# Gates and output products in pairs of pieces, in the order of the seven products

## The chip, the cores and the metric

One core of a Trainium2 chip runs the whole kernel. The metric is device microseconds of one execution; the median of the runs is compared.

## The reference

One inference step of a one-layer encoder trunk in float32, for 1024 prompt frames and 64 sample frames (1088 tokens) of width 1024:

```python
proj = xn @ w_in                                   # xn = rmsnorm(x), 1024 -> 5120
cb, cc, ch, q, k, v, ga, gb = jnp.split(proj, splits, axis=-1)
cv, conv_state = causal_conv(cc * ch, conv_prefix, w_conv)
ya = (cb * cv) @ w_conv_out                        # 512 -> 1024
o, new_k, new_v = attn_fn(heads(q), heads(k), heads(v))   # 8 heads of 64, chunk band
yb = o.reshape(B, L, ATT_DIM) @ w_attn_out         # 512 -> 1024
merged = jax.nn.sigmoid(ga) * ya + jax.nn.sigmoid(gb) * yb
x = x + merged @ w_out
x = x + (jax.nn.silu(h @ w1) * (h @ w3)) @ w2      # h = rmsnorm(x), 2816 hidden
return rmsnorm(x, g_final), ...
```

## The kernel before

Every float32 operand of a matmul is kept as two tiles of the fast format, a high part and the rest (`split`: a cast on ScalarE, then a subtraction on VectorE). A product is the sum of three matmuls: high weights by high data, high weights by the data's rest, the weights' rest by high data.

The 1088 tokens lie in columns: two halves of `HT` = 544 (512 prompt, 32 sample each), and each half is two pieces of `HN` = 272 columns, the width of one matmul. Channels are on the 128 partitions.

Most of the projection and the feed-forward go through `run`: a 2x2 block scheme with seven products instead of eight. It takes, for one block of weights, high weights by high data for both pieces of a half, high weights by the rest for both pieces, then the weights' rest by high data for both pieces (L266). Its operands are "quarter" tiles, in which a row block of 128 channels is `ROW` = 1152 floats long and the rest lies `HT + 8` = 552 floats behind the high part.

Twelve blocks of the two gates' projections (`GATES`: all eight of `ga` and the last four of `gb`) and the two output products `ya` and `yb` go through `product`, one piece of 272 columns at a time (L330 to L332). A gate has 8 row blocks, so 24 matmuls for a piece; an output has 4, so 12. `gate` copies each piece from PSUM (pool `pmm`, three banks) to a staging tile (`st_pool`, five) on ScalarE (L813), and GpSimd's queue stores it (L814).

The order of the program: the first halves of the first four gates (pieces 0 and 1), then the other pieces of these and five more gates, with about 2.7 steps of attention put between each two (`between`), then the last three gates (`LAST` = 3), when attention has ended. Ahead of these three the loads of `u` (the convolution branch) and `o` (attention, divided by its sums on VectorE and split into `ob`) are issued, and those of the gates. A planner that works through the program ahead of the run fixes the order of each engine's instructions: a later one may be placed ahead of one whose inputs or buffers it expects late. Gate matmuls stand singly among those of attention in the trace.

The outputs: for two blocks m of 128 channels `ya` (L1085 multiplies it by the sigmoid of `ga`), for the same two `yb` (L1095 multiplies, L1096 adds), and the sum is split into `mg` and, for the sample's columns, `ms`. Five banks of PSUM (`psum2`) hold pieces. Then the products with `w_out` follow, sample rows (from `ms`) first (L1143, L1144).

Weights: the high part lies in one of eight tiles of 512 (`ws`), the rest in one of eight slots of 512 in `low`, with an offset inside the slot (`at`): 0 for the gates and `run`, 40 for the outputs, 24 where the weights are the moving operand. `taken` counts the slots.

Of the kernel before, what the change touches and what calls it, by code (L numbers as in the profile page):

```python
# [8 lines left out]
F32 = mybir.dt.float32  # L9
# [46 lines left out]
class Acts:  # L56
# [3 lines left out]
        self.t = t  # L60

    def at(self, l, k, o, n):
        return self.t[:, l, k, o : o + n]


@with_exitstack
def encoder_kernel(ctx: ExitStack, tc: tile.TileContext, ins, outs):
# [58 lines left out]
    def split(hi, lo, src):  # L126

        a = act.copy(hi, src)  # L128
        b = vec.tensor_tensor(lo, src, hi.bitcast(F32), op=ALU.subtract)  # L129
        return a.ins, b.ins  # L130
# [192 lines left out]
    def product(out, w, x, o, n):  # L323

        kt = 4 * len(w)
        for k in range(kt):
            a, b = (t[:, k % 4] for t in w[k // 4])
            p, q = x.at(0, k, o, n), x.at(1, k, o, n)
            first, then = (q, p) if x is xn and o // HN % 2 == 0 else (p, q)
            mm(out, a, first, start=k == 0, stop=False)  # L330
            mm(out, a, then, start=False, stop=False)  # L331
            mm(out, b, p, start=False, stop=k == kt - 1)  # L332

    PIECES = [(j * HN, HN) for j in range(4)]
    GATES = [("a", m) for m in range(8)] + [("b", m) for m in range(4, 8)]
    for g, m in GATES:
# [468 lines left out]
    def gate(i, cs):  # L805
        g, m = GATES[i]
        dst = ga_d if g == "a" else gb_d
        for c in cs:
            o, n = PIECES[c]
            ps = pmm.tile([P, 512], F32, tag="mm", name=f"g{i}_{c}")  # L810
            product(ps[:, :n], gate_w[i], xn, o, n)
            st = st_pool.tile([P, HN], F32, tag="st", name=f"gst{i}_{c}")
            act.copy(st[:, :n], ps[:, :n])  # L813
            nc.gpsimd.dma_start(dst[m * P : (m + 1) * P, o : o + n], st[:, :n])  # L814
# [194 lines left out]
    sg = {}  # L1009

    def gates_in(nm, m):
        if nm == "gb":
            t = mp.tile([P, T], F32, tag="rc", name=f"gb{m}", bufs=3)
            nc.sync.dma_start(t, gb_d[m * P : (m + 1) * P])
            for o, n in PIECES:
                sg[nm, m, o] = t[:, o : o + n]
            return
        for o, n in PIECES:
            t = sg[nm, m, o] = mp.tile([P, HN], F32, tag=nm, name=f"{nm}{m}_{o}", bufs=8)
            nc.sync.dma_start(t, ga_d[m * P : (m + 1) * P, o : o + n])  # L1020

    head_load(0)

# [11 lines left out]
    for i in range(4, len(GATES)):  # L1035
        gate_w[i] = next_w()
        if i == len(GATES) - LAST:
            for _ in steps:
                pass
            att_stack.close()  # L1040
            uo = pg_stack.enter_context(tc.tile_pool(name="uo", bufs=1, reuse_waits="tile"))
            both_x = []
            for nm, pad in (("u", 56), ("ob", 48)):
                uo.tile([P, pad], F32, name=f"pad_{nm}")
                t = uo.tile([P, 2, 4 * T + 8], F32R, name=nm)[:, :, : 4 * T]
                both_x.append(Acts(t.rearrange("p l (k t) -> p l k t", k=4)))
            u, ob = both_x
            mp = pg_stack.enter_context(tc.tile_pool(name="mgp", bufs=4, reuse_waits="tile"))
            for k in range(4):
                if k == 3:  # L1050
                    gates_in("ga", 0)
                for q in {0: (0,), 1: (1,), 2: (), 3: (2, 3)}[k]:
                    nc.sync.dma_start(u.t[:, :, q].bitcast(F32), u_d[q])
                o = ob.t[:, 0, k].bitcast(F32)
                nc.sync.dma_start(o, o_d[k * P : (k + 1) * P])
                r = mp.tile([P, T], F32, tag="rc", name=f"rc{k}", bufs=3)
                for j in range(2):
                    src = rc_d[2 * k + j]
                    ld = nc.sync.dma_start(
                        r[j * HD : (j + 1) * HD], bass.AP(tensor=src.tensor, offset=src.offset, ap=[[0, HD], [1, T]])  # L1060
                    )
                vec.tensor_tensor(r, o, r, op=ALU.mult)
                split(ob.t[:, 0, k], ob.t[:, 1, k], r)
            with tc.issue_after(ld.ins):
                gates_in("ga", 1)
                gates_in("gb", 0)
        for c in range(4):
            gate(i, (c,))
            between()


    mg = quarters("mg")
    ms = mspool.tile([P, KD, 2, TS], F32R, tag="ms", name="ms")
    psum2 = pg_stack.enter_context(tc.tile_pool(name="psum2", bufs=5, space=PSUM, reuse_waits="tile"))
    for m0 in range(0, 8, 2):
        for m in (m0, m0 + 1):
            wa = next_w()
            if m0:
                gates_in("ga", m)
            for o, n in PIECES:  # L1080
# [4 lines left out]
                vec.tensor_tensor(t, ya[:, :n], t, op=ALU.mult)  # L1085
        for m in (m0, m0 + 1):
            wb = next_w()
            if m:
                gates_in("gb", m)
            for o, n in PIECES:  # L1090
                t, z = sg.pop(("ga", m, o)), sg.pop(("gb", m, o))
                act.activation(z, z, AF.Sigmoid)
                yb = psum2.tile([P, 512], F32, tag="mm", name=f"yb{m}_{o}")
                product(yb[:, :n], wb, ob, o, n)
                vec.tensor_tensor(z, yb[:, :n], z, op=ALU.mult)  # L1095
                vec.tensor_tensor(t, t, z, op=ALU.add)  # L1096
                split(mg.at(0, m, o, n), mg.at(1, m, o, n), t)
                h, a = o // HT, 512 - o % HT
                if a < n:
                    split(ms[:, m, 0, 32 * h : 32 * h + 32], ms[:, m, 1, 32 * h : 32 * h + 32], t[:, a:])  # L1100
    pg_stack.close()


# [62 lines left out]
    if True:  # L1166
# [557 lines left out]
```

## Time and profile before

| | |
|---|---|
| median of 3 runs | 1477.31 us (1476.44 to 1478.0) |
| the profiled execution | 1475.81 us, span 1473.8 us |
| granted TensorE clock | 0.999 |
| TensorE matmuls | 1458.0 us busy, 99% of the span, 10200 of them |
| VectorE, ScalarE, GpSimd busy | 979.2, 678.1, 133.1 us |
| HBM | 172.89 MB read, 91.92 MB written |

A matmul is shown with its whole way through the array, so that the next one starts before it ends; the distance from one start to the next tells what one costs. Lines name the kernel's source (L330 is line 330). Rows of the view by stretches give start and end in us, the length, then the busy time and number of instructions of each engine, the granted clock, the DMA engines' busy share and GB/s.

### The profile page before, as it was taken

The page shows a single profiled execution, that of the slowest core. Times are in us where ns is not written, and L with a number is a line of the kernel's source. Part 1 is how long each engine was busy: PE and PEld are TensorE (multiplying, and loading weights), DVE is VectorE, ACT ScalarE, POOL GpSimd, SP SyncE. Part 2 cuts the span into 40 slices and gives each one's busy share as a digit, 9 for nine tenths or more (in the row PEclk, how much of TensorE's full clock was granted, in tenths as well). Part 3 has the DMA queues.
Part 4 walks back from the last instruction along what each step waited for, and adds up shares of the span by engine and source line. Part 5 has one row for each costly group of instructions (what it writes and reads, how often), then busy time and mean ns, then how long its engine had stood idle before and what let it go on. Part 6 is the DMA issues. An engine that isn't in the chain of part 4 may idle for free.

```text
span 1473.8 us, 26481 instructions
## 1 busy us (share of the span) xinstructions
PE 1458.0 (99%) x10200; PEld 1369.7 (93%) x10200; DVE 979.2 (66%) x1850; ACT 678.1 (46%) x1396; POOL 133.1 (9%) x243
## 2 busy tenths in 40 slices
PE   8999999999999999999999999999999999999997
PEld 6899999999999999998889999999999999888886
DVE  7975465633776753763489767666666768957676
ACT  7644333434776753631355444444444445412223
POOL 1400010001111121000100111110011111000000
PEclk9999999999999999999999999999999999999999
DMA  8586523178766539544433454433344448777675
GB/s 292 177 271 224 177 93 113 60 212 233 190 191 176 152 101 326 186 126 136 147 114 108 147 183 162 161 140 120 119 149 159 149 161 308 256 233 248 212 268 203
DMA packets 164029, 264.72 MB, mean 180 GB/s; under 512 B 18624, under 2 KB 98688, under 8 KB 163872
## 3 DMA queue, kind: packets, MB, share of 16 engines
q1 hardware_dynamic: 143040, 196.13, 42.4%
q0 software_dynamic: 19712, 64.81, 12.2%
q10 hardware_dynamic: 1152, 2.10, 0.4%
q8 instruction: 80, 1.31, 0.4%
q14 instruction: 45, 0.37, 0.1%
HBM read 172.89 MB, written 91.92 MB: 180 GB/s over the span
## 4 chain that ended last, share of the span: by engine, by line
PE 92%; DVE 3%; DMA 2%; ACT 1%; SPq 1%; issue 1%; ACTq 0%; DVEq 0%
PE Ab L266 9%; PE Aa L266 8%; PE A L1637 8%; PE Db L266 4%; PE Da L266 4%; PE D L1637 4%; PE g L330 2%; PE g L331 2%; PE g L332 2%; PE B L1637 2%; PE Bb L266 2%; PE Ba L266 2%; PE wo L1139 2%; PE wo L1141 2%; PE wo L1140 2%; PE t L952 2%
## 5 line engine op out<-in xcount | busy, mean ns | idle before, releaser
L330 PE MATMUL g<-xn,wp 128*128 128x272 f32 x384 | 112.7, 293 | 0.0
L331 PE MATMUL g<-xn,wp 128*128 128x272 f32 x384 | 111.6, 291 | 0.0
L332 PE MATMUL g<-xn,low 128*128 128x272 f32 x384 | 110.6, 288 | 0.0
L128 ACT CAST ring<-w2r 128x512 fp32r<-128x512 f32 (+1 forms) x78 | 42.6, 587 | 89.0 <-PE A L1637 50.8
L128 ACT CAST hq<-sa 128x512 fp32r<-128x512 f32 x73 | 45.2, 620 | 81.0 <-DVE sa L1335 55.2
L863 DVE CUSTOM_DVE_ANT_0 p<-s,bb 128x640 f32<-128x640 f32 (+5 forms) x72 | 47.5, 661 | 42.5 <-DMA qd<-q_d 26.2
L1319 POOL DMA_DIRECT2D h_d<-hq x73 | 38.9, 533 | 400.4 <-DVE hq L129 230.7
L330 PEld LDWEIGHTS g<-xn,wp 128*128 128x128 f32 x384 | 72.3, 188 | 1.0
L332 PEld LDWEIGHTS g<-xn,low 128*128 128x128 f32 x384 | 72.3, 188 | 0.5
L331 PEld LDWEIGHTS g<-xn,wp 128*128 128x128 f32 x384 | 72.3, 188 | 0.1
L1637 PE MATMUL A<-ring,low 128*128 128x512 f32 x264 | 72.3, 389 | 0.0
L1637 PE MATMUL A<-ring,ht 128*128 128x512 f32 x264 | 72.2, 389 | 0.0
L129 DVE TENSOR_TENSOR hq<-sa,hq 128x512 fp32r<-128x512 f32 x73 | 50.3, 689 | 28.0 <-ACT hq L128 27.8
L129 DVE TENSOR_TENSOR low<-rawa,wa 128x512 fp32r<-128x512 f32 x55 | 37.7, 686 | 40.2 <-ACT wa L128 40.2
L1637 PEld LDWEIGHTS A<-ring,low 128*128 128x128 f32 x264 | 49.6, 188 | 10.3
L266 PE MATMUL Aa<-tt,wa 128*128 128x272 f32 x352 | 57.8, 285 | 1.3 <-ACT sa_Q L254 1.3
L1637 PEld LDWEIGHTS A<-ring,ht 128*128 128x128 f32 x264 | 49.5, 188 | 10.3
L266 PE MATMUL Aa<-mg,wa 128*128 128x272 f32 x352 | 57.8, 286 | 0.5 <-DVE sa L1300 0.5
L266 PE MATMUL Ab<-mg,wb 128*128 128x272 f32 x352 | 58.0, 286 | 0.0
L266 PE MATMUL Ab<-tt,wb 128*128 128x272 f32 x352 | 57.8, 285 | 0.0
L129 DVE TENSOR_TENSOR ring<-w2r,ring 128x512 fp32r<-128x512 f32 (+1 forms) x78 | 48.6, 645 | 11.1 <-ACT ring L128 10.9
L128 ACT CAST wa<-rawa 128x512 fp32r<-128x512 f32 x55 | 34.0, 620 | 47.0 <-PE Ab L266 33.3
(543 smaller groups left out, 4485.5 us busy)
## 6 DMA issues: line engine op xcount, KB each, us to landing
h_d<-hq POOLq DMA_DIRECT2D x73, 512.0 KB, 3.4
ht<-h_d SPq DMA_DIRECT2D x77, 256.0 KB, 3.6
low<-h_d SPq DMA_DIRECT2D x77, 256.0 KB, 3.6
rawa<-in_w_ff SPq DMA_DIRECT2D x11, 1024.0 KB, 5.7
rawb<-in_w_ff SPq DMA_DIRECT2D x11, 1024.0 KB, 5.3
w2r<-in_w_ff SPq DMA_DIRECT2D x11, 1024.0 KB, 7.0
qd<-q_d SPq DMA_DIRECT2D x32, 272.0 KB, 4.4
rawp<-in_w_in SPq DMA_DIRECT2D x6, 1024.0 KB, 6.3
```

Of the source, the lines that this page charges most:

```text
L128: a = act.copy(hi, src)
L129: b = vec.tensor_tensor(lo, src, hi.bitcast(F32), op=ALU.subtract)
L266: newest[0] = mm(t[:, j, :HN], w[:, k, :], x[p][:, k, l, j * HN : (j + 1) * HN], start=p in (1, 2, 7) and k == 0 and n == 0, stop=k == 3 a ...
L330: mm(out, a, first, start=k == 0, stop=False)
L331: mm(out, a, then, start=False, stop=False)
L332: mm(out, b, p, start=False, stop=k == kt - 1)
L863: vec.tensor_tensor_reduce(out=s if len(ps.shape) == 2 else s.rearrange("p (a b) -> p a b", a=2), in0=ps, in1=bias if len(ps.shape) == 2 e ...
L952: nc.tensor.transpose(tp[:, i * P : (i + 1) * P], s[:, i * P : (i + 1) * P], ident)
L1139: mm(ps, x(k, 0), wh, start=f, stop=False)
L1140: mm(ps, x(k, 1), wh, start=False, stop=False)
L1319: stored[0] = nc.gpsimd.dma_start(h_d[p, c - 1], hq.rearrange("p i l t -> p (i l t)").bitcast(F32)).ins
L1637: mm(t, ht[k][:, j, x], w[:, l], start=p in (1, 2, 7) and k == 0 and n == 0, stop=k == len(ks) - 1 and n == 2, skip_group_check=p in (6, 5 ...
```

## The change

- `product2` is new: two pieces at a time, into two PSUM banks, in the order of `run`. The outputs use it throughout; `gate` uses it when it is given two pieces, which is the case for the first halves of the first four gates and for the last three gates. The other gate pieces stay with `product`.
- An output product of a half takes one PSUM tile of two banks (`psum2`: two of them, four banks, instead of five of one bank), and the sigmoid, multiply, add and split work on 544 columns at once.
- `u` and `ob` are laid out anew: a row block is two halves of `HT + 32` floats, and the rest lies 4648 floats behind the high part. Their loads and the operations on them address halves; `u` is loaded in eight transfers instead of four, a `ga` block in two instead of four.
- The outputs' weights go to offset 0 in their slots of `low`, the skipped slot ahead of `w_out` (`taken[0] += 1`) is gone, and `st_pool` has three tiles instead of five.

```diff
 class Acts:
     def at(self, l, k, o, n):
-        return self.t[:, l, k, o : o + n]
+        h = o // HT
+        a = h * (HT + 32) + o - h * HT
+        return self.t[:, l, k, a : a + n]
+
+    def rows(self, l, k):
+        return self.t[:, l, k].rearrange("p (h t) -> p h t", h=2)[:, :, :HT]
...
+    def product2(outs, w, x, o):
+
+        kt = 4 * len(w)
+        for k in range(kt):
+            a, b = (t[:, k % 4] for t in w[k // 4])
+            for n, (s, l) in enumerate(((a, 0), (a, 1), (b, 0))):
+                for j in range(2):
+                    mm(
+                        outs[j], s, x.at(l, k, o + j * HN, HN),
+                        start=k == 0 and n == 0, stop=k == kt - 1 and n == 2,
+                    )
...
-            {"src": ins[nm][0][:, m * P : (m + 2) * P], "w": 2 * P, "at": 40}
+            {"src": ins[nm][0][:, m * P : (m + 2) * P], "w": 2 * P}
...
-    st_pool = pg_stack.enter_context(tc.tile_pool(name="st_pool", bufs=5, reuse_waits="tile"))
+    st_pool = pg_stack.enter_context(tc.tile_pool(name="st_pool", bufs=3, reuse_waits="tile"))
...
     def gate(i, cs):
         g, m = GATES[i]
         dst = ga_d if g == "a" else gb_d
-        for c in cs:
+        pss = [pmm.tile([P, 512], F32, tag="mm", name=f"g{i}_{c}") for c in cs]
+        if len(cs) == 2:
+            product2([ps[:, :HN] for ps in pss], gate_w[i], xn, PIECES[cs[0]][0])
+        else:
+            product(pss[0][:, :HN], gate_w[i], xn, *PIECES[cs[0]])
+        for c, ps in zip(cs, pss):
             o, n = PIECES[c]
-            ps = pmm.tile([P, 512], F32, tag="mm", name=f"g{i}_{c}")
-            product(ps[:, :n], gate_w[i], xn, o, n)
             st = st_pool.tile([P, HN], F32, tag="st", name=f"gst{i}_{c}")
...
+            for o in HALVES:
+                t = sg[nm, m, o] = mp.tile([P, HT], F32, tag=nm, name=f"{nm}{m}_{o}", bufs=4)
+                nc.sync.dma_start(t, ga_d[m * P : (m + 1) * P, o : o + HT])
...
-            for nm, pad in (("u", 56), ("ob", 48)):
+            for nm, pad in (("u", 24), ("ob", 24)):
                 uo.tile([P, pad], F32, name=f"pad_{nm}")
-                t = uo.tile([P, 2, 4 * T + 8], F32R, name=nm)[:, :, : 4 * T]
-                both_x.append(Acts(t.rearrange("p l (k t) -> p l k t", k=4)))
+                t = uo.tile([P, 8 * 2 * (HT + 32) + 40], F32R, name=nm)
+                n = 8 * (HT + 32)
+                t = bass.AP(tensor=t.tensor, offset=t.offset, ap=[t.ap[0], [n + 40, 2], [2 * (HT + 32), 4], [1, 2 * (HT + 32)]])
+                both_x.append(Acts(t))
...
-                    nc.sync.dma_start(u.t[:, :, q].bitcast(F32), u_d[q])
+                    for l in range(2):
+                        nc.sync.dma_start(u.rows(l, q).bitcast(F32), u_d[q, :, l].rearrange("p (h t) -> p h t", h=2))
...
-        for c in range(4):
-            gate(i, (c,))
-            between()
+        if i < len(GATES) - LAST:
+            for c in range(4):
+                gate(i, (c,))
+                between()
+        else:
+            gate(i, (0, 1))
+            gate(i, (2, 3))
...
-    psum2 = pg_stack.enter_context(tc.tile_pool(name="psum2", bufs=5, space=PSUM, reuse_waits="tile"))
+    psum2 = pg_stack.enter_context(tc.tile_pool(name="psum2", bufs=2, space=PSUM, reuse_waits="tile"))
...
-            for o, n in PIECES:
+            for o in HALVES:
                 t = sg["ga", m, o]
                 act.activation(t, t, AF.Sigmoid)
-                ya = psum2.tile([P, 512], F32, tag="mm", name=f"ya{m}_{o}")
-                product(ya[:, :n], wa, u, o, n)
-                vec.tensor_tensor(t, ya[:, :n], t, op=ALU.mult)
+                ya = psum2.tile([P, 2, 512], F32, tag="mm", name=f"ya{m}_{o}")
+                product2([ya[:, j, :HN] for j in range(2)], wa, u, o)
+                t = t.rearrange("p (j n) -> p j n", j=2)
+                vec.tensor_tensor(t, ya[:, :, :HN], t, op=ALU.mult)
...
         two_sums = early.tile([P, 2, D], F32, tag="raw", name="two_sums")
-        taken[0] += 1
         w = wo_half(0)
```

More of the change, by code (lines that the diff above doesn't have):

```diff
@@ L1009, in encoder_kernel @@
     sg = {}
+    HALVES = (0, HT)
     def gates_in(nm, m):
@@ L1014, in gates_in @@
             nc.sync.dma_start(t, gb_d[m * P : (m + 1) * P])
-            for o, n in PIECES:
-                sg[nm, m, o] = t[:, o : o + n]
+            for o in HALVES:
+                sg[nm, m, o] = t[:, o : o + HT]
             return
-        for o, n in PIECES:
-            t = sg[nm, m, o] = mp.tile([P, HN], F32, tag=nm, name=f"{nm}{m}_{o}", bufs=8)
-            nc.sync.dma_start(t, ga_d[m * P : (m + 1) * P, o : o + n])
+        for o in HALVES:
+            t = sg[nm, m, o] = mp.tile([P, HT], F32, tag=nm, name=f"{nm}{m}_{o}", bufs=4)
+            nc.sync.dma_start(t, ga_d[m * P : (m + 1) * P, o : o + HT])
     head_load(0)
@@ L1061, in encoder_kernel @@
                     )
+                r = r.rearrange("p (h t) -> p h t", h=2)
                 vec.tensor_tensor(r, o, r, op=ALU.mult)
-                split(ob.t[:, 0, k], ob.t[:, 1, k], r)
+                split(ob.rows(0, k), ob.rows(1, k), r)
             with tc.issue_after(ld.ins):
@@ L1089, in encoder_kernel @@
                 gates_in("gb", m)
-            for o, n in PIECES:
+            for o in HALVES:
                 t, z = sg.pop(("ga", m, o)), sg.pop(("gb", m, o))
                 act.activation(z, z, AF.Sigmoid)
-                yb = psum2.tile([P, 512], F32, tag="mm", name=f"yb{m}_{o}")
-                product(yb[:, :n], wb, ob, o, n)
-                vec.tensor_tensor(z, yb[:, :n], z, op=ALU.mult)
+                yb = psum2.tile([P, 2, 512], F32, tag="mm", name=f"yb{m}_{o}")
+                product2([yb[:, j, :HN] for j in range(2)], wb, ob, o)
+                z2 = z.rearrange("p (j n) -> p j n", j=2)
+                vec.tensor_tensor(z2, yb[:, :, :HN], z2, op=ALU.mult)
                 vec.tensor_tensor(t, t, z, op=ALU.add)
[L1097 to L1100, printed above, removed]
+                split(mg.at(0, m, o, HT), mg.at(1, m, o, HT), t)
+                h = o // HT
+                split(ms[:, m, 0, 32 * h : 32 * h + 32], ms[:, m, 1, 32 * h : 32 * h + 32], t[:, 512:])
     pg_stack.close()
```

6 lines of the change are left out of this document (3 added, 3 removed).

## The prediction

> **What bounds the kernel now.** I read the page first, then the waits of TensorE, then stretches of the span.
>
> ```profile
> span 1473.8 us, 26481 instructions
> PE 1458.0 (99%) x10200; PEld 1369.7 (93%) x10200; DVE 979.2 (66%) x1850; ACT 678.1 (46%) x1396; POOL 133.1 (9%) x243
> PE s L905 <- DVE mx L863: 0.5, 2, 0.3
> ```
>
> TensorE is busy for 99% of the span, and the longest wait that the view of its waits shows inside the part that is changed is half a microsecond (scores against the softmax). Nothing else can shorten the kernel much: a change pays only by fewer TensorE nanoseconds, and costs only where it makes TensorE wait. "Busy" hides something, though: a matmul is drawn with 0.29 us and the next starts long before it ends, so the price of one is the distance between starts. I read that from stretches in which TensorE runs one kind of matmul only, and divide by the number that the code issues.
>
> ```profile
> 302.41:308.33 5.92, 5.92 (x51) 5.92 (x49) 3.35 (x6) 3.19 (x7) 0.00 (x0) 1.00 0.93 304
> 323.13:347.08 23.95, 23.95 (x194) 23.95 (x193) 0.69 (x1) 3.78 (x9) 3.81 (x7) 1.00 0.91 271
> 543.48:573.42 29.94, 29.94 (x242) 29.94 (x241) 9.50 (x9) 10.43 (x20) 5.30 (x10) 1.00 0.95 317
> 575.04:671.07 96.03, 96.03 (x771) 96.03 (x769) 64.47 (x159) 45.79 (x126) 0.54 (x1) 1.00 0.53 164
> ```
>
> These are rows of the view by stretches: start and end, length, then PE, PEld, DVE, ACT, POOL busy (with counts that include what overlaps an edge), the granted clock (1.00 in all four), the DMA share. The rows are: two of the seven products of a projection unit (48 matmuls of 272 columns, 5.92/48 = 123.3 ns each); the first halves of the first four gates (192 matmuls, 23.95/192 = 124.7 ns); ten pieces of the last three gates (240 matmuls, 29.94/240 = 124.75 ns); the output products (768 matmuls, 96.03/768 = 125.0 ns). Shape, clock and weight loads are the same in all four. What differs is the order.
>
> ```profile
> 302.41 0.66 PE L266 MATMUL Agb<-xn,wgb 128*128 128x272 f32 x4
> 302.90 0.41 PE L266 MATMUL Agb<-xn,low 128*128 128x272 f32 x2
> 303.15 0.66 PE L266 MATMUL Agb<-xn,wgb 128*128 128x272 f32 x4
> 646.82 0.28 PE L331 MATMUL yb<-ob,wp 128*128 128x272 f32 x1
> 646.95 0.29 PE L332 MATMUL yb<-ob,low 128*128 128x272 f32 x1
> 647.07 0.29 PE L330 MATMUL ya<-u,wp 128*128 128x272 f32 x1
> ```
>
> The seven products take four matmuls with one weight block (two parts of the data, two pieces), then two with its low part, 0.74 us for the six. `product` takes three for one piece at a time.
>
> **The change, part by part.** *The order.* `product2` is the order of the seven products. For the gates the weights stay at offset 0 in `low` and `xn` stays where it is, so they become the stream of the first row. For the outputs the address of `u` and `o` matters too. Worked out from the code in floats mod 64 (256 bytes): a quarter tile has 552 = 40 between its two parts, 0 from row block to row block, 16 between pieces. The new tiles have 4648 = 40, 1152 = 0, 272 = 16 and 576 = 0 between halves; the old ones had 4360 = 8 between the parts. The base is the same as that of the first pass's sums: there 16 + 8 = 24 above a multiple of 64; here the pool of staging tiles shrinks from 5 to 3 times 272 (80 to 48 mod 64), and with the pad of 24 the sum is 24 again. So I take 123.33 ns for all. First four gates: 23.95 - 192 x 0.12333 = 0.27 us. Last three: 288 x (0.12475 - 0.12333) = 0.41 us. Outputs: 96.03 - 768 x 0.12333 = 1.31 us. Together 1.99 us, all of it on the path, since TensorE is the path. Bounds: 0 (the order does nothing) to 1.99.
>
> A rule speaks against it. The Trainium skill, "TensorE: Matmul & The Clock Gate", section "Back-to-back issue gap", gives N/2.4 + 2.5 ns between warm single matmuls, 115.8 ns for 272 columns, with no term for order or address. By it this part would be worth 0; the trace already disagrees, with 123.3 and 125.0 ns for one shape at one clock.
>
> *Evictions twice as wide.* Two operations of 272 columns become one of 544.
>
> ```profile
> L1085 DVE TENSOR_TENSOR ga<-ya,ga 128x272 f32<-128x272 f32 x32 | 13.9, 438 | 21.7 <-PE ya L332 21.7
> L128 ACT CAST mg<-ga 128x272 fp32r<-128x272 f32 x32 | 13.3, 416 | 18.6 <-DVE ga L1096 18.5
> L1328 DVE TENSOR_TENSOR sa<-Ab,sa 128x544 f32<-128x544 f32 x11 | 7.9, 718 | 0.0
> L128 ACT CAST scr<-scr 128x544 fp32r<-128x544 f32 x16 | 10.4, 647 | 14.1 <-DVE scr L703 9.5 <-issue 2.2 <-DVE scr L577 1.9
> ```
>
> One of 544 costs 0.72 us on VectorE and 0.65 us on ScalarE against 2 x 0.44 and 2 x 0.42: less work, but each chain gets longer. That matters in two places.
>
> The tail. The first `w_out` product (the sample rows) wants the last slice of `ms`.
>
> ```profile
> 671.07 0.40 PE L1143 MATMUL wo<-low,ms 128*128 128x512 f32 x1
> 674.31 0.40 PE L1143 MATMUL wo<-low,ms 128*128 128x512 f32 x1
> 671.27 0.44 DVE L1095 TENSOR_TENSOR gb<-yb,gb 128x272 f32<-128x272 f32 x1 [0.25 <-PE yb L332]
> 673.28 0.18 DVE L129 TENSOR_TENSOR ms<-ga,ms 128x32 fp32r<-128x32 f32 x1
> 673.38 0.68 DVE L129 TENSOR_TENSOR wo<-wor,low 128x512 fp32r<-128x512 f32 x1
> ```
>
> Now `ms` is ready at 673.46, and the fifteenth matmul wants it at 674.31. With 544 columns: multiply 671.27 to 671.99, add to 672.71, cast to 673.39, split to about 674.1, `ms` to 674.3; the matmul's weights are loaded some 0.2 us ahead, and a split of `wo` (0.68) may come in between. Wait 0.2 to 0.8 us; I take 0.4.
>
> Two PSUM tiles instead of five. Each holds a half now, so the multiply has to be done one half (2.96 us) after its products end.
>
> ```profile
> 599.07 0.29 PE L330 MATMUL ya<-u,wp 128*128 128x272 f32 x1
> 601.60 0.43 DVE L1095 TENSOR_TENSOR gb<-yb,gb 128x272 f32<-128x272 f32 x1
> ```
>
> The last piece of the first pair of `yb` was complete at 599.07 and multiplied only until 602.03, 2.96 us later: VectorE is behind there with late weight splits. That is exactly the new limit, so 0 to 1.5 us once; I take 0.3. Elsewhere VectorE waits for TensorE (21.7 us in the row of L1085 above).
>
> *Loads.* Four loads of `u` become eight of half the size, eight of `ga` become four: the same 25 issues on SyncE's queue before the outputs and the same bytes. `u` is wanted 18 matmuls after the first output product instead of 9, as both pieces walk the rows together: 1.1 us more room. I cost this at nothing; if it is late, the price is the delay of the last `u` tile, below 1 us.
>
> *Staging tiles, 5 to 3, and PSUM tiles of the gates.*
>
> ```profile
> 326.01 0.29 PE L332 MATMUL g<-xn,low 128*128 128x272 f32 x1
> 326.33 0.39 ACT L813 COPY gst<-g 128x272 f32<-128x272 f32 x1 [2.12 <-PE g L332]
> DMA to landing us min/median/max: 2.3/4.2/8.0
> ```
>
> A staging tile is held for its copy, the way to the queue and the landing, 5 to 9 us, and two are wanted per 5.92 us. The copy of a second piece can so wait on ScalarE up to some 2.5 us, ahead of casts and sigmoids queued behind it; the bank it empties is wanted one pair later, so TensorE doesn't see it. `pmm` keeps three banks, and pairs take two: the second bank of a pair is the first of the pair before, free 0.32 + 0.39 = 0.71 us after the last start into it, while its first matmul is due 3 x 0.123 = 0.37 us after that. A wait of 0.34 us, at most 0.53 with a weight load of 0.19 behind it, at 3 + 5 pairs that follow a pair. If the planner orders the matmuls of the free bank ahead, as it interleaves single matmuls of gates with attention now, little is left: I take 0.2 in all, and the full price is the first rival.
>
> *Sum:* -1.99 + 0.4 + 0.3 + 0.2 = -1.1 us. The profiled execution took 1475.81 us (2.0 around its span), 1.5 below the median of the three runs; I take the difference over to the median: 1477.31 - 1.1 = **1476.2 us**.
>
> **The rivals.** *The pairs wait for their bank.* If the order inside `product2` is kept as written, eight pairs wait 0.34 to 0.53 us: 2.7 to 4.2 us in place of 0.2, 1478.7 to 1480.2 us, slower. It decides from 0.25 us per pair, where it eats the gain. For it: three banks and the copy's row. Against it: gate matmuls are now split up in the trace among scores and transposes, so the order isn't the program's.
>
> *Order does nothing*, and the seven products owe their gap to something else: the 1.99 us fall away, 1478.2 us. Against it: the rows of 123.3 and 125.0, one shape at one clock. The section of the Trainium skill named above would have it so.
>
> *The attention stretch is laid out anew.* Between 347 and 541 us gates fill the holes of the heads in an order fixed before the run; with pairs, three staging tiles and other copy times that order can shift.
>
> ```profile
> 354.74 0.29 PE L330 MATMUL g<-xn,wp 128*128 128x272 f32 x1
> 355.08 0.51 PE L905 MATMUL s<-kd,qd 128*128 128x512 f32 x1
> 510.85 0.29 PE L330 MATMUL g<-xn,wp 128*128 128x272 f32 x1
> 511.26 0.44 PE L952 MATMUL t<-ident,p 128*128 128x128 f32 x2
> ```
>
> These are the first and the last of sixteen places there where the next start comes 0.15 us or more later than is usual for the shape; together 3.9 us. Half gone, or half more, is 2 us either way: 1474.2 or 1478.2 us; all gone, 1472.3.
>
> **How the numbers follow.** What a measurement of this kernel can tell from no change is about 0.2%, 2.95 us: 1474.36 to 1480.26. Chances: forecast 0.45 (own range 1475.3, nothing lost, to 1477.8, with the upper bounds of both VectorE waits); pairs wait 0.22; order does nothing 0.08; attention better 0.15, worse 0.10. Faster by over 0.2%: nearly all of attention better and a twentieth from the forecast, 0.20. Slower by over 0.2%: the pairs' wait at its upper bound or together with a worse attention stretch, 0.15. Within: 0.65. The range leaves out the far ends of attention better and of the pairs' wait: 1473.7 to 1480.3.
>
> **What would show it.** The outputs' stretch is 94.7 us (123.3 ns per matmul) and the first gates' 23.7: order right; 96 and 24: wrong. A hole of 0.3 us or more at the second matmul of a pair of gates: first rival. A gap ahead of the fifteenth `w_out` matmul, waiting for `ms`: the tail. TensorE waiting for the multiply of `yb` near 590 to 604 us: two PSUM tiles are too few. The forecast is wrong if the stretch from 347 to 541 us changes by more than 2 us, or if `u` lands after TensorE wants it.

## The result, and the profile after

The change made the kernel slower by 3.0 us: 1480.62 us median (1477.97 to 1485.12, 21 runs) against 1477.6 us (1475.02 to 1480.22, 21 runs) of the kernel before on the same chip, ratio 1.002 with a 95% interval of 1.0012 to 1.0027. The forecast was 1476.2 us, its range ended at 1480.3 us, and 0.15 was given to this side.

The page of the changed kernel begins:

```profile
span 1478.3 us, 26323 instructions
PE 1461.7 (99%) x10200; PEld 1370.7 (93%) x10200; DVE 973.9 (66%) x1786; ACT 673.3 (46%) x1348; POOL 133.1 (9%) x243
```

The profiled execution took 1480.29 us, 4.5 above the one of before. TensorE has the same 10200 matmuls and 3.7 us more of "busy". As in the prediction, busy time says little; the stretches between the starts of the same matmuls do. These are rows of the view by stretches of the kernel before: the first gates, the gates behind the attention, the way from `w_out` to the up phase of the feed-forward part (its first half, before the down phase), and the up phase itself.

```profile
323.13:350.08 26.95, 26.95 (x218) 26.95 (x217) 0.69 (x1) 4.17 (x10) 4.35 (x8) 1.00 0.92 269
541.99:575.04 33.05, 33.05 (x265) 33.05 (x265) 10.33 (x11) 10.94 (x21) 5.97 (x11) 1.00 0.93 312
671.07:772.74 101.67, 101.67 (x474) 83.34 (x473) 53.00 (x111) 37.23 (x74) 9.25 (x17) 1.00 0.44 144
772.74:1233.85 461.11, 458.76 (x3714) 457.91 (x3713) 327.70 (x550) 213.65 (x404) 45.38 (x85) 1.00 0.42 150
```

And the same view of the changed kernel, the outputs in third place (96.03 us before):

```profile
322.91:350.45 27.54, 27.52 (x219) 26.91 (x218) 0.69 (x1) 3.88 (x10) 4.32 (x8) 1.00 0.93 268
542.80:576.98 34.18, 34.14 (x265) 33.08 (x265) 10.93 (x12) 11.65 (x21) 5.44 (x10) 1.00 0.94 299
576.98:671.93 94.95, 94.95 (x771) 94.81 (x769) 57.02 (x95) 40.64 (x80) 1.08 (x2) 1.00 0.51 161
671.93:774.44 102.51, 102.14 (x475) 83.20 (x474) 53.24 (x111) 36.76 (x72) 9.26 (x17) 1.00 0.43 143
774.44:1238.60 464.16, 460.81 (x3713) 459.53 (x3712) 327.94 (x550) 213.70 (x404) 45.38 (x85) 1.00 0.42 149
```

The outputs gained 1.08 us, as forecast. The first gates lost 0.59, the last gates 1.13, the attention stretch between them (350.08 to 541.99 before, 350.45 to 542.80 after) 0.44, `w_out` and what follows it 0.84. That is +1.92 us in the stretch that was edited. The up phase, whose instructions stand in the same order on every engine in both kernels, took 3.05 us more in this execution. The down phase that follows took 231.7 us in both.

Where the gates lost: one boundary between two pairs, in the timeline of TensorE, and the copy of ScalarE that empties the bank the next pair wants.

```profile
328.21 0.53 PE L346 MATMUL g<-xn,wp 128*128 128x272 f32 x3
328.58 0.41 PE L346 MATMUL g<-xn,low 128*128 128x272 f32 x2
328.83 0.41 PE L346 MATMUL g<-xn,wp 128*128 128x272 f32 x2
329.08 0.29 PE L346 MATMUL g<-xn,low 128*128 128x272 f32 x1
329.34 0.52 PE L346 MATMUL g<-xn,wp 128*128 128x272 f32 x2
```

```profile
328.90 0.39 ACT L833 COPY gst<-g 128x272 f32<-128x272 f32 x1 [4.91 <-PE g L346]
```

The pair ends with the two matmuls at 328.58. The order fixed ahead of the run did put the three matmuls of the free bank in front (328.83, 328.95 and 329.08), as the forecast hoped. But the copy (0.39 us, begun at 328.90) is over only at 329.29, and the first matmul into that bank starts 0.05 us later, at 329.34: 264 ns after the one before instead of 123, and the next gap is 234. So this boundary costs 0.25 us (0.14 and 0.11) although the matmuls were reordered. All eight boundaries show the same, at 0.25 to 0.29 us each, 2.15 us together; in every one the matmul starts 0.05 us after the copy's end.

The tail, on VectorE, with the `w_out` matmul that waited:

```profile
672.13 0.72 DVE L1127 TENSOR_TENSOR gb<-yb,gb 128x544 f32<-128x544 f32 x1
672.78 0.69 DVE L134 TENSOR_TENSOR wo<-wor,low 128x512 fp32r<-128x512 f32 x1
673.39 0.72 DVE L1128 TENSOR_TENSOR ga<-ga,gb 128x544 f32<-128x544 f32 x1
674.82 0.72 DVE L134 TENSOR_TENSOR mg<-ga,mg 128x544 fp32r<-128x544 f32 x1 [0.71 <-ACT mg L133]
675.47 0.18 DVE L134 TENSOR_TENSOR ms<-ga,ms 128x32 fp32r<-128x32 f32 x1
```

```profile
675.71 0.50 PE L1174 MATMUL wo<-low,ms 128*128 128x512 f32 x1 [0.37 <-DVE ms L134]
```

The chain is the one forecast, with a split of `wo` (672.78) inside it and VectorE idle for 0.71 us while ScalarE casts 544 columns. The matmul at 675.71 starts 0.77 us after the one before it (674.93), where 0.23 is usual, and one gap of 0.34 us follows.

### The profile page after: what moved, and what is told of

Its sections match the earlier page's. It is cut to its first block, busy times and chain, and to the rows that moved or that the text cites. A ratio compares the mean times of both kernels' runs of the same rounds, so it can differ in the third digit from the quotient of the medians.

```text
span 1478.3 us, 26323 instructions
## 1 busy us (share of the span) xinstructions
PE 1461.7 (99%) x10200; PEld 1370.7 (93%) x10200; DVE 973.9 (66%) x1786; ACT 673.3 (46%) x1348; POOL 133.1 (9%) x243
## 4 chain that ended last, share of the span: by engine, by line
PE 68%; issue 23%; DMA 3%; DVE 2%; ACT 2%; POOL 1%; SPq 1%; POOLq 0%; ACTq 0%; DVEq 0%
PE A L1667 8%; PE Ab L271 6%; PE Aa L271 5%; PE D L1667 4%; PE Db L271 3%; PE Da L271 3%; PE g L346 2%; PE B L1667 2%; PE t L972 2%; PE pv L997 2%; PE Ak L271 2%; PE Aq L271 2%; PE g L336 2%; PE Acc L271 2%; PE Acb L271 2%
## 5 line engine op out<-in xcount | busy, mean ns | idle before, releaser
L335 PE MATMUL g<-xn,wp 128*128 128x272 f32 x224 | 66.6, 297 | 0.0
L336 PE MATMUL g<-xn,wp 128*128 128x272 f32 x224 | 65.7, 293 | 0.0
L337 PE MATMUL g<-xn,low 128*128 128x272 f32 x224 | 64.7, 289 | 0.0
L893 ACT ACTIVATE p<-p,mx 128x640 f32<-128x640 f32 (+5 forms) x72 | 50.8, 706 | 10.0 <-DVE mx L883 8.5
L346 PE MATMUL g<-xn,wp 128*128 128x272 f32 x320 | 55.3, 290 | 0.1
L271 PEld LDWEIGHTS Aa<-tt,wa 128*128 128x128 f32 x352 | 49.2, 189 | 3.0 <-ACT sa_Q L259 2.9
```

The costliest lines, as they stand in the source:

```text
L271: newest[0] = mm(t[:, j, :HN], w[:, k, :], x[p][:, k, l, j * HN : (j + 1) * HN], start=p in (1, 2, 7) and k == 0 and n == 0, stop=k == 3 a ...
L346: mm(outs[j], s, x.at(l, k, o + j * HN, HN), start=k == 0 and n == 0, stop=k == kt - 1 and n == 2,)
L893: act.activation(s, s, AF.Exp, bias=mx, scale=-1.0, accum_out=sm)
```

## The experiments

Times are medians of the run; ratios are against the kernel before on the same chip. "Gates to outputs", "outputs", "to the up phase" and "up phase" are lengths between the same matmuls as above: 251.91, 96.03, 101.67 and 461.11 us before; 254.07, 94.95, 102.51 and 464.17 after.

**The pairs' banks.** e1_banks gives each pair of gates one two-bank tile, from the pool of the attention (first four gates) or of the outputs (last three gates).

```diff
-        pss = [pmm.tile([P, 512], F32, tag="mm", ...) for c in cs]
         if len(cs) == 2:
+            pool, tag = (patt, "att") if i < 4 else (psum2, "mm")
+            two = pool.tile([P, 2, 512], F32, tag=tag, ...)
+            pss = [two[:, j] for j in range(2)]
             product2(...)
```

> The changed kernel, but a pair of gate pieces takes one PSUM tile of two banks that nobody else holds (of the scores' pool for the first four gates, of the outputs' pool for the last three) instead of two of three single banks. Theory A (the waits of the second piece for its bank, eight times 0.25 us, and the slower rhythm of the pairs after them are what the change lost): no wait at the second matmul of a pair, 123.3 ns in all pairs, the stretch from the first gate to the first output product 251.3 us (251.9 before, 254.1 changed), the time 1.0 to 1.5 us below the kernel before, ratio 0.9991. Theory B (the loss comes from the outputs, their two PSUM tiles and the new layout): as the changed kernel, 2 to 3 us above.

1480.16 us, ratio 1.0024 (1.0010 to 1.0038); gates to outputs 253.18, outputs 95.27, to the up phase 102.57, up phase 462.48.

```profile
323.49:350.30 26.81, 26.81 (x216) 26.81 (x217) 0.16 (x1) 2.79 (x8) 4.32 (x8) 1.00 0.95 257
612.74:671.94 59.20, 59.20 (x483) 59.20 (x481) 36.64 (x62) 22.64 (x46) 0.00 (x0) 1.00 0.39 120
```

```profile
PE rt L958 <- DVE pt L134: 1.5, 1, 1.5
PE g L346 <- ACT scr L592: 1.0, 1, 1.0
```

The first 216 gate matmuls fall from 27.54 to 26.81 us: no boundary waits, and every pair runs at 123.3 ns, like 480 matmuls of the outputs (59.20 us). So the waits were for banks. The second fence, from the waits of TensorE, says why the time didn't follow: the borrowed banks are still held, at one end by the projections (1.0 us), at the other by the attention. There, near 538 us, 13 matmuls of the last gates fill the attention's own wait for a split in the changed kernel; here they can't start yet, and TensorE waits 1.5 us. The wait moved. (f1 below, which leaves the first pair of either kind in the old banks, has neither of the two.)

**Single gates.** e2_single_gates keeps everything but the pairs of gates.

```diff
-        gate(i, (0, 1))
+        gate(i, (0,))
+        gate(i, (1,))
```

> The changed kernel with all gate pieces through the old product, one at a time; the outputs stay in pairs. Theory A: gates as before, outputs 94.8 us, 0.4 us lost ahead of the w_out products: 0.5 to 0.9 us below the kernel before, ratio 0.9995. Theory B: 2 to 3 us above it.

1479.77 us, ratio 1.0021 (1.0007 to 1.0035); gates to outputs 252.19, outputs 96.77, to the up phase 102.35, up phase 463.99. The gates' loss is gone, and the outputs now lose what they had gained:

```profile
PE ya L346 <- DMA u<-u_d: 1.2, 1, 1.2
PE ya L346 <- DVE ga L1117: 0.3, 1, 0.3
```

The outputs start 2.35 us earlier here (574.63 instead of 576.98), and the last part of `u` isn't there. The loads of `u`, in the view of one tile, before and (second fence) after:

```profile
L1053 SPq DMA_DIRECT2D u<-u_d x4: 549/573/592, 544.3 to 566.0; - x4
DMA to landing us min/median/max: 5.7/9.8/11.0
```

```profile
L1078 SPq DMA_DIRECT2D u<-u_d x8: 359/415/578, 545.1 to 567.6; - x8
DMA to landing us min/median/max: 3.9/10.2/11.0
```

The last of the eight transfers is issued at 567.6 instead of 566.0. In e2 it is issued at 567.8, and the matmul that wants it starts only at 578.69, 10.9 us later. In the changed kernel the outputs begin just late enough, thanks to the gates' waits. So a second wait, of 1.2 us, lay hidden behind the first.

**Gates alone.** e3_gates_only is the kernel before with pairs of gates and nothing else (`product2` in `gate`, `gate(i, (0, 1))` and `gate(i, (2, 3))` for the last three).

> The kernel before with the gates' pairs alone (three PSUM banks, five staging tiles; outputs, u and o as before). Theory A: eight waits of 0.25 us and the pairs' rhythm, against 0.3 us gained: 1.5 to 2 us above the kernel before, ratio 1.0012, outputs 96.0 us. Theory B: the gates gain up to 0.7 us: 0 to 0.7 us below.

1480.0 us, ratio 1.0019 (1.0009 to 1.0028); gates to outputs 253.58, outputs 96.01, to the up phase 101.73, up phase 465.02. The pairs of gates cost 1.67 us of the edited stretch by themselves, where the forecast had a gain of 0.68 and a wait of 0.2.

**The kernel before again.** b0_before and b1_before are the kernel before, unchanged.

> The kernel before once more, for a second profile. From the end of the outputs on, all engines' instructions are in the same order in both kernels, yet the changed kernel's profile has lost 2.9 us between 860 and 960 us, after two late snapshots. Theory A takes this for chance: a second profile of before may show such stretches of 125.5 ns too, in other places. If it is the change's doing, this profile shows none.

> The kernel before against itself, to learn what a comparison of this kernel is worth. If only the text of the program counts: ratio 1.000 with an interval of 0.001 to either side. If building or placing a program anew shifts it (its one profile more took 1483.3 us): a ratio off 1 by 0.001 to 0.003, and then the same share of the changed kernels' 0.2% is no doing of the change.

b0_before took 1483.34 us in its one execution; each part of its edited stretch was within 0.12 us of before (251.79, 96.03, 101.71), its up phase 467.52 us. b1_before took 1476.82 us, ratio 0.9993 (0.9983 to 1.0003), up phase 461.19. So the up phase of one and the same program varies by 6 us between executions. The 3 us between the medians of 21 executions each are still no matter of chance (0.12% to 0.27%, where before against itself had -0.17% to 0.03%).

**Banks, loads and tail together.** f1_banks_u_tail is e1 with the first pair of either kind in the old banks, the loads of `u` one head earlier, and the last half multiplied, added and split piece by piece.

```diff
-                for q in {0: (0,), 1: (1,), 2: (), 3: (2, 3)}[k]:
+                for q in {0: (0, 1), 1: (2,), 2: (3,), 3: ()}[k]:
...
+                if (m, h) == (7, 1):
+                    for j in (1, 0):
+                        c = slice(j * HN, (j + 1) * HN)
+                        vec.tensor_tensor(z[:, c], yb[:, j, :HN], z[:, c], op=ALU.mult)
+                        vec.tensor_tensor(t[:, c], t[:, c], z[:, c], op=ALU.add)
...
```

> The changed kernel with three repairs: the first pair of gate pieces of each stretch stays in the gates' own banks, the others take two-bank tiles that nobody holds; the last two loads of u are issued one step earlier each (ahead of o's and the gates'); the very last half of yb is multiplied, added and split piece by piece, the piece with the sample columns first. Theory A (bank waits, the later landing of u's last tile and the wait for ms are all that the change loses up to the w_out products): first gate to first output product 251.3 us, outputs 94.9, w_out to the feed-forward 101.8 us, together 1.7 us less than before; the feed-forward's up phase, which has varied from 461.1 to 467.5 us over profiles with the same order of instructions, decides how much of it the time shows: ratio 0.999 if that phase is as often disturbed as before. Theory C (the shift or the moved weight slots make the up phase slower by a lasting 1.5 us or so): gates, outputs and w_out as said, yet the time not below before's: ratio 1.000 to 1.001.

1480.59 us, ratio 1.0025 (1.0011 to 1.0038); gates to outputs 251.59, as expected, but outputs 101.63 and to the up phase 103.06.

```profile
PE ya L346 <- ACT gst L839: 5.1, 1, 5.1
PE wo L1185 <- DVE xr L1207: 1.1, 1, 1.1
```

```profile
582.49 0.39 ACT L839 COPY gst<-g 128x272 f32<-128x272 f32 x1 [7.11 <-DMA gb_d<-gst]
```

With the gates on time and their banks shared with the outputs, the second pair of the outputs waits 5.1 us until ScalarE has copied the last gates out. The second fence, from the timeline of ScalarE, says why the copy is late: it waits 7.1 us for one of the three staging tiles, whose store has not landed. The piecewise end doesn't help either: VectorE is behind, and now `w_out` waits for the sum that empties its bank (`xr`).

**Which part of the order counts.** e4_old_distances is e1 with the old distances of `u`, `o` and the weights' low parts; e5_old_order (second diff) is e1 with the new distances and `product` for the outputs, `yb` like `ya`.

```diff
-            {"src": ..., "w": 2 * P}
+            {"src": ..., "w": 2 * P, "at": 40}
-                t = bass.AP(..., ap=[t.ap[0], [n + 40, 2], ...])
+                t = bass.AP(..., ap=[t.ap[0], [n + 8, 2], ...])
```

```diff
-                product2([ya[:, j, :HN] for j in range(2)], wa, u, o)
+                [product(ya[:, j, :HN], wa, u, o + j * HN, HN) for j in range(2)]
```

> Pairs of gates in two-bank tiles, outputs in the pairs' order, but u and o with the old distance between their two parts (8 floats mod 64 instead of 40) and the outputs' weights at offset 40 again. If the order alone gives the rhythm of 123.3 ns: ya 11.84 us per 96 matmuls. If the addresses matter: above 11.9, up to 12.0.

> Pairs of gates in two-bank tiles, u and o and the weights at the new addresses, but the outputs piece by piece through the old product. If the order alone gives the rhythm: 12.0 us per 96 matmuls. If the addresses alone do: 11.84.

One execution each (1481.86 and 1480.08 us). 480 matmuls of the outputs, e4 and then e5:

```profile
614.66:674.66 60.00, 60.00 (x482) 60.00 (x481) 35.54 (x61) 22.20 (x45) 0.00 (x0) 1.00 0.38 119
```

```profile
613.38:673.24 59.86, 59.86 (x482) 59.86 (x481) 35.53 (x61) 22.07 (x45) 0.00 (x0) 1.00 0.38 119
```

125.0 and 124.7 ns against 123.3 (59.20 us) with both, in the same banks and with the same evictions. Neither the order nor the distances alone bring the outputs to 123.3. One execution is little, since one stream can run in two rhythms (p1_one_tile, below); but e4's gaps repeat one and the same pattern before and behind its two stalls, so there it isn't a stall that chose the slower one.

**Without the feed-forward part.** c_before_front and c_after_front end behind the attention's residual.

```diff
+    turned(*late.pop(0))
+    turned(*late.pop(0))
...
+        nc.sync.dma_start(dst, x1_d[t0 : t0 + n])
...
+    return
     operands = {p: ax[gh] for p, gh in PLAIN.items()} | tt
```

> The kernel before without its feed-forward part: it ends when the residual rows behind the outputs are stored, and copies those rows out. Its time is only a base for the next run. From the stages of the profile of before (start of the up phase at about 773 us) it should take 775 to 785 us. The part that is left out begins with an identical order of instructions in both kernels, so what before and after differ by here is what the change does in the stretch that it edits, in all executions and not in one profile.

> The changed kernel without its feed-forward part, as the run before it. Theory A (the edited stretch itself costs it: +2.2 us gates, -1.1 us outputs, +0.8 us tail in the two profiles) expects the median 1.9 us above that of c_before_front, within 0.5 us; the other 1.1 us of the 3.0 us measured then come from the feed-forward part, where TensorE falls into its slower rhythm more often. Theory B (the edited stretch loses more in most executions than in the one that was profiled) expects 2.7 us or more. Theory C (the difference is made in the feed-forward part alone) expects 0.5 us or less.

791.98 us (791.08 to 792.48) and 793.38 us (792.51 to 794.81); of the difference of 1.4 us, a 95% interval by resampling the four and five times reaches from 0.5 to 3.3. Theory A had 1.9 within 0.5 and is met at its edge; C is out by the median, hardly by the interval; B isn't excluded by these few runs. The two profiled executions have one and the same span, since `u` came late in the one of before:

```profile
PE ya L330 <- DMA u<-u_d: 1.3, 1, 1.3
```

```profile
PE wo L1174 <- DVE ms L134: 0.4, 1, 0.4
```

The first row is of c_before_front, the second of c_after_front, both from the waits of TensorE. The loads of `u` have no room to spare in the kernel before either: in this execution they missed.

**Single gates, loads earlier, tail piecewise.** e9_best joins the edits of e2 and of f1's loads and tail.

> The changed kernel with all gates in single pieces, the u transfers started one head earlier each, and the multiply, add and split of the very last half done piece by piece, the one with the sample columns first. If the losses are those that the runs so far showed (pairs of gates waiting for a bank 2 us, u landing late 1.2 us, ms late 0.4 to 0.8 us), gates to outputs take 252.0 us, the outputs 95.1 and the way to the up phase 101.8, together 0.7 us less than before, and the time is about 1477 us where before has 1477.6. Rival: u started earlier only pushes the loads of the last heads back, and attention or the staging of the gates pays; then gates to outputs take 253 us or more and the time is 1479 us or more.

1480.22 us, ratio 1.0013 (1.0002 to 1.0024); gates to outputs 252.23, outputs 96.43, to the up phase 103.08, up phase 464.65. The wait for `u` is gone, but in its place stand others for VectorE:

```profile
PE wo L1180 <- DVE xr L1202: 1.1, 1, 1.1
PE yb L346 <- DVE ga L1117: 0.7, 1, 0.7
PE ya L346 <- DVE ga L1117: 0.4, 1, 0.4
```

The expectation for the outputs (95.1) was 1.3 us too low, the one for the tail (101.8) as much.

**One tile.** p1_one_tile has the banks of f1 with one two-bank tile instead of two, so that every pair of the outputs waits for the eviction of the one before.

```diff
-    psum2 = ... tc.tile_pool(name="psum2", bufs=2, ...)
+    psum2 = ... tc.tile_pool(name="psum2", bufs=1, ...)
```

> As e1_banks with one two-bank tile instead of two for the last gates and the outputs, so that every pair waits for the eviction of the pair before: some 20 stalls of 0.6 to 1.3 us on purpose. Question: which rhythm follows a stall (123.3 or 125.5 ns for one stream of instructions). If the rhythm is drawn anew at each stall, both show up among these pairs, 11.84 and 12.05 us per 96 matmuls once the stall is taken off; if the rhythm depends on the stage only (addresses, instruction order), all the pairs of the outputs show one of the two. Outputs take 96.0 + 12 to 18 us in all.

Outputs 131.4 us: 31 stalls of about 1.0 us, more than the twenty that were expected. Between the stalls 22 matmuls run freely. The view by stretches, 18 gaps of each of three such pairs, and the last 12 gaps of the third pair:

```profile
590.71:592.97 2.26, 2.26 (x21) 2.26 (x19) 0.53 (x1) 0.56 (x2) 0.00 (x0) 1.00 0.33 73
594.81:597.03 2.22, 2.22 (x21) 2.22 (x20) 0.53 (x1) 1.83 (x3) 0.00 (x0) 1.00 0.47 147
598.85:601.09 2.24, 2.24 (x21) 2.24 (x20) 0.00 (x0) 0.00 (x0) 0.00 (x0) 1.00 0.00 0
599.73:601.21 1.48, 1.48 (x15) 1.48 (x13) 0.00 (x0) 0.00 (x0) 0.00 (x0) 1.00 0.00 0
```

2.26/18 = 125.6 ns, then 123.3 and 124.4, and 1.48/12 = 123.3 (from starts in ns: 125.6, 123.3, 124.1 and 123.3). The third pair begins more slowly and settles into the rhythm of the second. So there are two lasting rhythms for one stream of instructions at clock 1.00, one gap pattern for each (121, 128, 119, 122, 125, 125 ns and 126, 124, 126, 124, 125, 128 ns, give or take one). Of the 31 pairs behind a stall 27 end in the first, 8 of them from the start and 19 after some 8 to 16 slower gaps; 4 keep the second up to the next stall. Which one follows isn't plain chance: the pairs behind stalls 4 to 7 and those behind stalls 8 to 11 have the same gaps, one for one.

**A fourth buffer.** In the up phase a cast of ScalarE needs one of three `hq` buffers, each held until its block is stored; a late store holds up the cast, the snapshot behind it, and TensorE, which wants the snapshot. d_before4 and d_after4 have four (the room comes from the `early` pool). The wait in the changed kernel, in the timelines of ScalarE and TensorE:

```profile
955.81 0.62 ACT L133 CAST hq<-sa 128x512 fp32r<-128x512 f32 x1 [3.75 <-DMA h_d<-hq]
```

```profile
960.14 0.77 PE L271 MATMUL Aa<-tt,wa 128*128 128x272 f32 x4 [1.01 <-ACT sa_Q L259]
```

```diff
-    early = ctx.enter_context(tc.tile_pool(name="early", bufs=1, ...))
-                hq = hp.tile(..., tag="hq", bufs=3)
+                hq = hp.tile(..., tag="hq", bufs=4)
-            self.raw = (early if kp == blocks[1][0] else rpool).tile(...)
+            self.raw = rpool.tile(...)
```

> The kernel before with four buffers instead of three for the split hidden blocks that wait for their store. If the waits of the up phase (TensorE for a snapshot, behind a cast that waits for a buffer) are what most executions of before lose over its undisturbed profile (median 1477.6, undisturbed 1475.3 to 1475.8), this takes 1475.5 us or less, ratio 0.9985, and its up phase 461 us. If they are rare in before, it is the same as before.

> The changed kernel with the same fourth buffer. Theory A (of the 3.0 us, 1.4 to 1.9 are lost in the edited stretch, the rest in the up phase's waits for a buffer, which the changed kernel meets more often) expects it 1.4 to 1.9 us above d_before4, with an up phase of 461 us. Theory B (the up phase is slower for another reason, such as the slow rhythm without any wait) expects 3 us above d_before4.

1478.13 us, ratio 1.0009 (0.9997 to 1.0022), and 1479.78 us, ratio 1.0012 (1.0003 to 1.0021); up phase 461.11 us in both. ScalarE's waits for the stores in before, after, d_before4 and d_after4, a fence for each, and in the last two also TensorE's waits in the down phase:

```profile
ACT hq L128 <- DMA h_d<-hq: 13.6, 11, 2.0
```

```profile
ACT hq L133 <- DMA h_d<-hq: 17.3, 12, 3.7
```

```profile
ACT hq L128 <- DMA h_d<-hq: 8.4, 5, 2.3
PE A L1636 <- ACT acc L1646: 1.3, 2, 1.0
```

```profile
ACT hq L133 <- DMA h_d<-hq: 7.6, 5, 2.0
PE A L1666 <- ACT acc L1676: 2.0, 3, 0.9
```

The fourth buffer halves those waits and gives the changed kernel an undisturbed up phase, but the down phase pays (234.0 and 234.8 us instead of 231.7), so neither kernel gets faster. The difference of the two medians is 1.65 us, in the 1.4 to 1.9 that theory A gave; resampled, it lies between 0 and 2.6, which leaves out theory B's 3 us. (The ratios, in which one run of d_before4 at 1485.74 us weighs, differ by less, 0.0003.)

**Outputs alone, five banks.** g1_single keeps single gates and gives each output piece a bank of its own with its own multiply; g2_single4 adds the fourth buffer.

```diff
-                ya = psum2.tile([P, 2, 512], F32, tag="mm", ...)
-                product2([ya[:, j, :HN] for j in range(2)], wa, u, o)
+                ya = [psum2.tile([P, 512], F32, tag="mm", ...)[:, :HN] for j in range(2)]
+                product2(ya, wa, u, o)
```

> Outputs alone in pairs, each pair in two banks of five with an eviction per piece, the piece with the sample columns first; gates single as before, u started one head earlier. If the losses seen so far are the waits for banks, for u and for ms, none of them is left and only the gain of the outputs' order stays: outputs 94.8 us, the way to the up phase 101.7, in all 1.2 us less than before in these stretches; 1476.4 us where before has 1477.6, unless the up phase is disturbed more often (then up to 1478.5).

> g1_single with the fourth buffer. If both theories hold, it is 1.2 us below d_before4, about 1474.3 us; if the fourth buffer does nothing, it is as g1_single.

1477.84 us, ratio 1.0004 (0.9993 to 1.0014), and 1478.22 us, 1.0007 (0.9998 to 1.0016): no difference from before that can be told. g1's stretches: 252.23, 96.17, 102.76, up phase 461.50.

```profile
PE ya L346 <- DVE gb L1131: 1.0, 1, 1.0
PE wo L1174 <- DVE xr L1196: 0.7, 1, 0.7
```

The order's 1.3 us are earned at 123.3 ns and given back: a pair wants two banks at once, and VectorE, which near 600 us first waits 1.5 us for a cast of ScalarE and then has a weight split in its way, empties them late. No version tried beats the kernel before.

## Why the prediction was wrong

**The order: right for the outputs, paid away for the gates.** 94.95 us measured, 94.7 forecast plus 0.3 for a wait of TensorE for VectorE. Such a stall is there, 0.2 us at 606.7, but behind a multiply of `ya` (605.91 to 606.63), not of `yb`. The argument with distances mod 64 floats held: 123.3 ns in the undisturbed stretches of all nine profiles that had both order and distances and two tiles or more, 125.0 in all six with neither (e4 and e5 stand between). Pairs of gates run at 123.3 too, in e1 throughout and in the changed kernel between the boundaries; but three boundaries cost more than that gains, so the first gates lost 0.59 us where 0.27 gained were forecast. The rival "order does nothing" is out. The Trainium skill, "TensorE: Matmul & The Clock Gate", section "Back-to-back issue gap", has in its formula for single matmuls one gap per number of columns, 115.8 ns here; the rows show 123.3 to 125.5 for one shape at one clock.

**The pairs' wait for a bank: the step that failed.** The prediction took 0.2 us for all eight boundaries, 0.025 each, if the free bank's matmuls go first. They did, and by the prediction's own figures that leaves 0.71 - 5 x 0.123 = 0.09 us, not 0.025. Measured: the copy ends 0.71 us after the last start into the bank (328.58), as forecast, the next matmul into it starts another 0.05 later, 0.14 late, and the gap behind it is 0.11 too long. The way from the copy's end to the matmul and the slow gap after the stall weren't priced. So the eight boundaries cost 2.15 us where 0.2 were forecast. Rival 1 had the mechanism, though not its condition, since the order wasn't kept as written. Its threshold, 0.25 us per pair, weighs the waits against the 1.99 us alone; with the 0.7 us that the sum gives to the tail and the two tiles, 0.16 is enough. That its time, 1478.7 to 1480.2 us, comes so near the measured 1480.62 is partly chance, since the tail and the up phase add to it and the outputs' gain is in both.

**The tail: right in kind, half its size.** 0.84 us instead of 0.4. The chain was laid out in the prediction link by link, and the wait for `ms` itself, 0.54 us, lies inside its 0.2 to 0.8: the split of `wo` that may come in between did, and the chain took 3.52 us from the multiply's start to the end of `ms` instead of 3.03. The slow gap behind the stall (0.11 us) wasn't priced, and the rest, 0.2 us, comes in small steps further on in the stretch.

**The loads: costed at nothing, hidden by something else.** The prediction counted issues and bytes, both right, and not where in the queue the last issue stands: 567.6 instead of 566.0 us. In the changed kernel the gates' waits hid it; take them away and 1.2 us show (e2). An edit costed at nothing needs its cover named, and the cover here was another loss. The three staging tiles were likewise taken as unseen by TensorE; that held in the changed kernel, but in f1 the wait for one of them stood behind 5.1 us.

**The attention stretch** changed by 0.44 us, well within the 2 us; that rival didn't come about.

**The up phase: not in the prediction at all.** It was taken as unchanged, since nothing in it is edited. Of the 3.0 us, the edited stretch accounts for 1.4 to 1.9 (1.92 in the profiles, 1.4 without the feed-forward part, 1.65 with the fourth buffer). The rest arises in executions in which the up phase waits for stores. In the profiled one a gap of 1.3 us between two starts (ended at 960.14) and 81 us in a slow rhythm are most of the 3.05 us. Among the profiles of kernels with three buffers, two of three of before, but of the ten of changed forms of it only those of e4, e5 and g1, stayed within 0.5 us of 461.1. The moved weight slots aren't the reason: e3 has the old ones and 465.02 us, e5 the new ones and 461.11. Why the changed forms meet the late store more often, with the same order of instructions, isn't settled; that they do is an observation on few profiles.

## What to carry to other kernels

On an engine that is busy for 99% of the time, a cheaper order of instructions is worth only what the buffers around it let through: count how many matmuls of cover lie between the last write into a bank and the next, against the eviction, the way from its end to the next start, and the slow gap behind a stall. When a loss is taken away, the next limit can be within a microsecond or so (here `u`, then VectorE): read its slack off the trace before costing an edit at nothing. And compare single profiles by stage, since one program's up phase differed by 6 us between executions.

## What the runs showed of the hardware

TensorE has two lasting rhythms for one stream, in the up phase as in p1_one_tile. Within one execution of the changed kernel, 480 matmuls each of the up phase:

```profile
885.01:945.28 60.27, 60.27 (x482) 60.27 (x481) 38.93 (x66) 25.33 (x48) 5.78 (x11) 1.00 0.38 133
970.11:1029.31 59.20, 59.20 (x482) 59.20 (x481) 38.62 (x65) 25.28 (x49) 4.81 (x9) 1.00 0.34 123
```

125.6 ns and 123.3 ns, at clock 1.00. The slow stretch begins at a stall of 0.2 us near 875 us and ends at the next, near 958 us; 81 us of it cost 1.4 us. Short stalls thus can have two prices: their own length, and the rhythm of everything up to the next one. In b0_before the slow rhythm held for some 280 us. What sets which rhythm follows a stall was not found.

A bank is written again only a little after the copy out of it has ended: at all eight boundaries of the changed kernel, and at all eight of e3, the matmul started 0.05 us after that, and the gap behind it was 0.23 us instead of 0.12.
